# Hybrid decoder layer: part of the MLP's weight sums from transfers to VectorE, and an input loaded earlier and split later

## The chip, the cores and the metric

The kernel runs on one core of a Trainium2 chip. The metric is the device time of one execution in microseconds (us), as the median of several runs. The profile is one further execution, recorded by the hardware.

The engines are called as the profile calls them: PE is TensorE (matrix products; PEld is its loading of the stationary operand), DVE is VectorE, ACT is ScalarE, POOL is GpSimd, SP is the engine that issues most transfers. SBUF is the on-chip memory with 128 partitions, PSUM holds the products of TensorE in eight banks, DRAM is the large memory beside the core.

## The reference

One layer of a decoder for 512 tokens of 1024 numbers, all in fp32:

```python
proj = x @ w_in                                    # q, k, v of three mixers, and three gates
merged = (g[:, :, 0] * (o_da @ w_branch_da) + g[:, :, 1] * (o_sb @ w_branch_sb)
          + g[:, :, 2] * (o_dl @ w_branch_dil))    # g = sigmoid(gates)
x = layer_norm(DEEPNORM_ALPHA * x + merged @ w_out, ln1_g[i], ln1_b[i])
hid = jax.nn.relu(x @ w_up[i])                     # 1024 -> 4096
c = jnp.square(hid) @ w_down[i]                    # 4096 -> 1024
ple = jax.nn.sigmoid(x @ w_ple_gate[i]) * (p[i] @ w_ple[i])
x = layer_norm(DEEPNORM_ALPHA * x + c + ple, ln2_g[i], ln2_b[i])
```

`o_da`, `o_sb` and `o_dl` are a differential attention, a stick-breaking attention and a dilated sliding-window attention. For what follows the three products with large weights matter: the gates, the per-layer embedding (`ple`, with its input `p`) and the MLP (`w_up`, `w_down`).

## The kernel before

**Products in three parts.** Every fp32 operand of a large product is split into a high part (a cast to a shorter float, by ScalarE) and a low part (the remainder, by VectorE). The product is high times high, high times low and low times high, three matmuls that add up in a PSUM bank. For weights this is `split_next` (lines 239 to 262): ScalarE writes `wh` (line 255), VectorE writes `wl` (line 258). A weight block is 128 partitions x 1024 numbers, 512 KB.

**Buffers.** Raw blocks are loaded by SP into a ring of 5 (`RAW`, line 223), the split blocks lie in a ring of 7 (`RING`). `fill` issues the next load only when the block five loads earlier has no further use. `pump` splits ahead as far as `freed + RING` allows; `freed` grows by the blocks that an item lists as done.

**Items.** The work of TensorE is a list of items, each a group of matmuls with an eviction of its result. The loop at the end of `trunk` goes through them in order; at each item it evicts the result before, splits weights, calls hooks and may issue a transfer. The list has 59 items of projections, three gates of 14 items with the 8 items of branch 2 in front of the third gate, then the 8 items each of branch 0 and branch 1 (`first_branch` is the first of these), 8 of the output projection (`wout_at`), 22 of the embedding's gate and the embedding, and the MLP. The order of instructions within each engine's queue is set when the program is built; it follows the items by and large, with some instructions ahead of or behind their item.

**Seven products instead of eight.** The gates, the embedding's gate and the MLP multiply in blocks of two by two, with seven products (numbered 1 to 7) of sums of blocks instead of eight products of plain blocks. The four blocks of such a group are a quad here. Products 1, 2 and 3 use three raw blocks; products 4, 5, 6 and 7 use sums of blocks. The MLP has 15 quads: 8 of `w_up` and 7 of `w_down`; the last part of `w_down` is multiplied plainly.

**Where the sums are made.** `totals` (lines 149 to 174) puts them into two queues: `copies` (SP copies a raw block within DRAM, line 186) and `sums` (POOL starts a transfer that adds a block to the copy, line 190). A plain quad takes 4 copies and 4 sums and then loads 7 blocks: 3 raw ones and 4 sums. A mixed quad (`mixed=True`) takes 2 copies and 2 sums, for products 5 and 7; products 6 and 4 are then made by VectorE in place on the raw block of product 5: once it is split for product 5, another raw block is added to it (line 244). It loads 5 blocks. Gates 1 and 2 have mixed quads, gate 0, the embedding's gate and the whole MLP plain ones.

**When the sums are made.** The loop counts units of work (4 for a projection, 2 for a gate or a branch item) and calls `add` once per `rate` units. `add` takes a copy while fewer than 24 copies lead, else a sum. Until item 23 only copies are made. One sum waits for a cast three casts back, which spreads them.

**The MLP.** `mlp_items` takes `up` quad 0, then seven pairs of `up` quad b+1 and `down` quad b. `up_item` and `down` are its items, in the order of products 1, 2, 6, 5, 7, 3, 4 for `up`, and by the string `order` for `down`.

**The input p.** `load_pT` (lines 1250 to 1256) is called at item `first_branch + 6`. It loads the two halves of `pT` by SP, and at once casts each by ScalarE (line 1254) and subtracts by VectorE (line 1255). In the items around it `halves` (lines 571 to 575, hooked to `first_branch + 4` to `+ 7`) splits the four operands `oTh`, `oTl` of branch 1, by ScalarE and VectorE in turn for the cast (lines 93 and 95). The embedding's items (lines 784 to 806), which use the split `pT`, come after the output projection.

Of the kernel before, what the change touches and what calls it, by code (L numbers as in the profile page):

```python
# [52 lines left out]
def trunk(tc, a, out):  # L53
    nc = tc.nc
    es = ExitStack()
    with es:
# [92 lines left out]
        def totals(quads, mixed=False):  # L149

            def new():
                return dram.tile([P, 1024], F32, name=nm("total"), tag=nm("total"), bufs=1)

            if mixed:
                t = [(new(), new()) for _ in quads]
                for o in range(2):
                    for q, x in zip(quads, t):
                        copies.append((x[o], q[3 * o]))
                for o in range(2):
                    for q, x in zip(quads, t):  # L160
                        sums.append((x[o], q[1]))
                return [{1: q[0], 2: q[2], 3: q[3], 5: x[0], 7: x[1]} for q, x in zip(quads, t)]
            t = [[new() for _ in range(4)] for _ in quads]
            for o, i in ((0, 0), (2, 1), (1, 3), (3, 2)):
                for q, x in zip(quads, t):
                    copies.append((x[o], q[i]))
            for o, i in ((0, 1), (2, 3)):
                for q, x in zip(quads, t):
                    sums.append((x[o], q[i]))
            for o in (1, 3):  # L170
                for x in t:
                    sums.append((x[o], x[o // 2][:, :]))
            return [{1: q[0], 2: q[2], 3: q[3], 4: x[3], 5: x[0], 6: x[1], 7: x[2]} for q, x in zip(quads, t)]
# [658 lines left out]

        def mlp_items():
            nb = 7
            up_w, down_w = {}, {}

            def weights(b):
                q = [[a["wu"][b, i].rearrange("p j k m -> p (j k m)") for i in range(4)]]
                if b:
                    q.append([a["wd"][b - 1, i].rearrange("p k n -> p (k n)") for i in range(4)])  # L840
                w = totals(q)
                up_w[b] = w[0]
                if b:
                    down_w[b - 1] = w[1]
# [11 lines left out]
                nc.scalar.activation(t, src, AF.Relu)  # L856
                nc.scalar.activation(t, t, AF.Square)

            def up_item(b, p):
                c = chunk(up_w[b][p], 1024)  # L860

                def bank():
                    if p in (1, 2, 5):
                        held["A" if p == 1 else "B"] = mm_bank()
                    return held["B" if p in (2, 5, 3) else "A"]

                def mm(ps):
                    for j in range(2):
                        o = ps[:, 256 * j:256 * j + 256]
                        for k in range(4):  # L870
                            s = slice((4 * j + k) * P, (4 * j + k) * P + P)
                            h, lo = operand(x1_ops, p, k, slice(0, 256))
                            first = j == 0 and k == 0 and p in (1, 2, 5)
                            last = j == 1 and k == 3 and p in (2, 3, 4)
                            nc.tensor.matmul(o, c["h"][:, s], h, start=first, stop=False, skip_group_check=True)  # L875
                            nc.tensor.matmul(o, c["h"][:, s], lo, start=False, stop=False, skip_group_check=True)  # L876
                            nc.tensor.matmul(o, c["l"][:, s], h, start=False, stop=last, skip_group_check=True)  # L877

                def ev(ps):
                    if p in (1, 5, 6):  # L880
                        t = slot("cut")
                        nc.scalar.copy(t, ps)
                        cut[p] = t
                        return
                    if p == 2:
                        t = cut.pop(1)
                        nc.vector.tensor_add(t, t, ps)  # L887
                        squared(t, t)
                        n = 11
                    elif p == 7:  # L890
                        t = cut.pop(5)
                        nc.vector.tensor_sub(t, t, ps)
                        squared(t, t)
                        n = 22
                    elif p == 3:
                        t = cut.pop(6)
                        nc.vector.tensor_sub(t, ps, t)
                        squared(t, t)
                        n = 12
                    else:  # L900
                        t = slot("hid")
                        squared(t, ps)
                        n = 21
                    hid[b, n] = t
                    if n == 21:
                        jobs_of(b)
                item([c], mm, ev, need=[c], bank=bank, size=2)

            hid = {}

# [158 lines left out]
                    part(3, half, cc)  # L1069

            def ups(b):
                for p in (1, 2, 6, 5, 7, 3, 4):
                    up_item(b, p)
                    extra[len(items) - 1] = 2 if b == 1 else 1

            def downs(b):
                w = down_w[b]
                c = {}

                def go(p, r):  # L1080
                    if p not in c:
                        c[p] = chunk(w[p], 1024)
                    down(b, p, r, c[p], [c[p]] if r else [])

                order = "20 10 21 11 50 60 51 30 61 31 70 40 71 41" if b < nb - 1 else "10 11 50 60 51 61 70 71"
                for x in order.split():
                    go(int(x[0]), int(x[1]))
                if b == nb - 1:
                    for p in (2, 3, 4):
                        c[p] = chunk(w[p], 1024)  # L1090
                    return [c[p] for p in (2, 3, 4)]
# [157 lines left out]

        def load_pT():  # L1250
            for k in range(2):
                raw, h, lo = slot("pT"), slot("pTh", F32R), slot("pTl", F32R)
                nc.sync.dma_start(raw, a["pT"][:, k, :])
                nc.scalar.copy(h, raw)
                nc.vector.tensor_sub(lo, raw, h.bitcast(F32))
                pTs[k] = (h, lo)
# [336 lines left out]
        for n, it in enumerate(items):  # L1593
# [27 lines left out]
                turn_da()  # L1621
            if n >= 7 and not wout_at + 5 <= n < wout_at + 20 and not gates_at - 2 <= n < gates_at + 2:
                due[0] += it["size"]
                rate = 2.3 if n < gates_at else 5 if n < gates_at + 14 else 3 if n < first_branch else 2.2 if n < wout_at else 5.5
                while due[0] >= rate:
                    due[0] -= rate
                    add(n < 23)
            if n == first_branch + 6:
                load_pT()
            if n == wout_at - 6:  # L1630
                ln_consts("ln1_g", "ln1_b")
                for tt in range(4):
                    load_xn(tt)
# [110 lines left out]
```

## Time and profile before

| what | value |
|---|---|
| median of 3 runs | 1085.56 us (1085.28 to 1085.81) |
| the profiled execution's own time | 1085.31 us |
| its span in the profile | 1083.6 us |
| VectorE's casts and subtractions of weights, line 258 | 245, 296.5 us busy |
| copies within DRAM (SP) | 84 of 512 KB |
| adding transfers (POOL) | 84 of 512 KB |
| moved in all | 227.99 MB, 210 GB/s in the mean |

The span runs from the first to the last recorded instruction; the execution's own time is 1.7 us longer. Busy time is the time in which an engine executes; register, branch and transfer-issuing instructions are not counted in it. A row of waits reads: engine, instruction waiting, what ended the wait, then the total in us, how often, and the longest. A row of a timeline reads: start in us, duration, engine, line, operation, output and inputs, and in square brackets the idle time of the engine before it with what ended it. In the chain of waits each row is start, duration and what was running.

### The profile page before, as it was taken

How to read it: one execution, taken by the hardware profiler on the slowest of the kernel's cores; microseconds unless marked ns; L12 is line 12 of the kernel's file. 1: busy time of each engine (PE TensorE's matmuls, PEld its weight loads, DVE VectorE, ACT ScalarE, POOL GpSimd, SP SyncE). 2: the span in 40 equal slices, each digit the busy share in tenths (PEclk: the TensorE clock that was granted, in tenths of full speed). 3: DMA queues.
4: the chain of work that ended last, by engine and by line, in shares of the span. 5: the costliest groups of instructions: out<-in, count | busy, mean ns of one | idle time of the engine just before them, and what ended most of it. 6: DMA issues, size and time to landing. Idle time of an engine off the chain costs nothing.

```text
span 1083.6 us, 14812 instructions
## 1 busy us (share of the span) xinstructions
PE 1049.7 (97%) x5503; PEld 899.6 (83%) x5503; DVE 761.1 (70%) x1316; ACT 558.8 (52%) x908; POOL 98.1 (9%) x119
## 2 busy tenths in 40 slices
PE   9999999999999899999999969999999999999996
PEld 6877788999888688888887748877999889989985
DVE  6888566646354578887747745798786886787786
ACT  6566445333333446777536212275666566567551
POOL 0000101010211100111101100100001010110000
PEclk9999999999999899999999979999999999999999
DMA  7455564628979975475967984348779889898612
GB/s 272 155 214 184 206 251 91 144 97 214 271 205 310 272 224 175 116 214 160 321 176 248 289 301 136 109 140 260 252 237 285 250 243 280 233 273 237 224 68 78
DMA packets 69516, 227.99 MB, mean 210 GB/s; under 512 B 8077, under 2 KB 11037, under 8 KB 68100
## 3 DMA queue, kind: packets, MB, share of 16 engines
q1 hardware_dynamic: 45220, 179.97, 45.3%
q0 software_dynamic: 23648, 46.17, 24.3%
q8 instruction: 43, 0.70, 0.2%
q10 hardware_dynamic: 576, 0.92, 0.2%
q14 instruction: 29, 0.24, 0.1%
HBM read 224.90 MB, written 90.20 MB: 291 GB/s over the span
## 4 chain that ended last, share of the span: by engine, by line
PE 93%; DVE 3%; DMA 2%; ACT 1%; issue 1%; SPq 0%; POOL 0%; DVEq 0%; ACTq 0%
PE mm L84 6%; PE mm L85 6%; PE mm L86 6%; PE mm L875 5%; PE mm L876 5%; PE mm L877 5%; PE mm L363 3%; PE mm L365 3%; PE mm L364 3%; PE at L453 3%; PE at L454 3%; PE at L451 3%; PE mm L963 2%; PE mm L962 2%; PE mm L964 2%; PE mm L598 2%
## 5 line engine op out<-in xcount | busy, mean ns | idle before, releaser
L255 ACT CAST wh<-raw 128x1024 fp32r<-128x1024 f32 x245 | 255.4, 1050 | 242.4 <-PE mm L876 41.7
L258 DVE TENSOR_TENSOR wl<-raw,wh 128x1024 fp32r<-128x1024 f32 x245 | 296.5, 1222 | 117.4 <-ACT wh L255 114.1
L84 PE MATMUL mm<-xhT,wh 128*128 128x512 f32 x304 | 122.0, 401 | 1.3 <-DVE da_qb L105 1.1
L85 PE MATMUL mm<-xlT,wh 128*128 128x512 f32 x304 | 119.9, 394 | 0.0
L86 PE MATMUL mm<-xhT,wl 128*128 128x512 f32 x304 | 119.8, 394 | 0.0
L875 PE MATMUL mm<-XH,wh 128*128 128x256 f32 x256 | 72.6, 284 | 2.6 <-DVE cut L887 1.4
L876 PE MATMUL mm<-XL,wh 128*128 128x256 f32 x256 | 72.4, 283 | 0.0
L877 PE MATMUL mm<-XH,wl 128*128 128x256 f32 x256 | 72.4, 283 | 0.0
L84 PEld LDWEIGHTS mm<-xhT,wh 128*128 128x128 f32 x304 | 57.6, 190 | 15.3 <-issue 3.9
L86 PEld LDWEIGHTS mm<-xhT,wl 128*128 128x128 f32 x304 | 57.4, 189 | 12.2 <-DVE wl L258 0.3
L85 PEld LDWEIGHTS mm<-xlT,wh 128*128 128x128 f32 x304 | 57.7, 190 | 10.8
L363 PE MATMUL mm<-wh,xhT 128*128 128x512 f32 x160 | 64.2, 402 | 0.0
L190 POOL DMA_DIRECT2D total<-total x38 | 33.7, 894 | 328.2 <-ACT wh L255 286.1
L365 PE MATMUL mm<-wh,xlT 128*128 128x512 f32 x160 | 63.2, 395 | 0.0
L364 PE MATMUL mm<-wl,xhT 128*128 128x512 f32 x160 | 63.2, 395 | 0.0
L877 PE MATMUL mm<-xs,wl 128*128 128x256 f32 x192 | 54.3, 283 | 0.0
L875 PE MATMUL mm<-xs,wh 128*128 128x256 f32 x192 | 54.3, 283 | 0.0
L876 PE MATMUL mm<-xs,wh 128*128 128x256 f32 x192 | 54.3, 283 | 0.0
L875 PEld LDWEIGHTS mm<-XH,wh 128*128 128x128 f32 x256 | 49.1, 192 | 3.5 <-issue 1.6
L598 PE MATMUL mm<-wh,oTh 128*128 128x512 f32 x96 | 38.9, 405 | 12.9 <-DVE oTh L95 12.9
L876 PEld LDWEIGHTS mm<-XL,wh 128*128 128x128 f32 x256 | 49.1, 192 | 0.2
L877 PEld LDWEIGHTS mm<-XH,wl 128*128 128x128 f32 x256 | 49.1, 192 | 0.0
(421 smaller groups left out, 2550.2 us busy)
## 6 DMA issues: line engine op xcount, KB each, us to landing
raw<-total SPq DMA_DIRECT2D x84, 512.0 KB, 5.8
raw<-in_wt_dram SPq DMA_DIRECT2D x38, 512.0 KB, 7.4
total<-total POOLq DMA_DIRECT2D x38, 512.0 KB, 9.5
total<-in_wu_dram SPq DMA_DIRECT2D x32, 512.0 KB, 9.1
total<-in_wd_dram SPq DMA_DIRECT2D x28, 512.0 KB, 9.0
raw<-in_wd_dram SPq DMA_DIRECT2D x25, 512.0 KB, 5.3
raw<-in_wu_dram SPq DMA_DIRECT2D x24, 512.0 KB, 6.1
raw<-in_wv_dram SPq DMA_DIRECT2D x20, 512.0 KB, 4.0
```

The lines of the kernel that those rows point to most:

```text
L84: nc.tensor.matmul(ps, wh, xh, start=start, stop=False, skip_group_check=True)
L85: nc.tensor.matmul(ps, wh, xl, start=False, stop=False, skip_group_check=True)
L86: nc.tensor.matmul(ps, wl, xh, start=False, stop=stop, skip_group_check=True)
L255: i = nc.vector.tensor_copy(h, raw) if c.get("dve") else nc.scalar.copy(h, raw)
L258: i = nc.vector.tensor_sub(lo, raw, h.bitcast(F32))
L363: nc.tensor.matmul(ps, x1, c["h"][:, s], start=k == 0, stop=False)
L364: nc.tensor.matmul(ps, x1, c["l"][:, s], start=False, stop=False)
L365: nc.tensor.matmul(ps, x2, c["h"][:, s], start=False, stop=k == 7)
L598: nc.tensor.matmul(ps, h[:, q], c["h"][:, s], start=k == 0, stop=False)
L875: nc.tensor.matmul(o, c["h"][:, s], h, start=first, stop=False, skip_group_check=True)
L876: nc.tensor.matmul(o, c["h"][:, s], lo, start=False, stop=False, skip_group_check=True)
L877: nc.tensor.matmul(o, c["l"][:, s], h, start=False, stop=last, skip_group_check=True)
```

## The change

Quads of `up` 2, 4 and 6 and of `down` 1, 3 and 5 become mixed. `mixed_chunks` loads their five blocks (products 1 and 2, or 2 and 1, then 5, 3, 7) and splits in the order first two, 5, 6, 4, 3, 7, where 6 is block 5 with block 3 added and 4 is that with block 2 added. As this is not the order of the items, it also says which split blocks each item gives back: 5 and 6 after product 5 (in `down` after each), and 4, 3 and 7 after product 4. The rates of `add` change, and the input `pT` is loaded at `first_branch + 3` and split at `first_branch + 14`.

```diff
         def mlp_items():
             nb = 7
+            MIXED = (2, 4, 6)
             up_w, down_w = {}, {}
+
+            def mixed_chunks(w, first):
+                raw = {q: load(w[q], 1024) for q in (*first, 5, 3, 7)}
+                c = {p: chunk_of(raw[{6: 5, 4: 5}.get(p, p)], {6: raw[3], 4: raw[2]}.get(p))
+                     for p in (*first, 5, 6, 4, 3, 7)}
+                return c, {6: [], 5: [c[5], c[6]], 7: [], 3: [], 4: [c[4], c[3], c[7]]}
...
-                w = totals(q)
+                w = totals(q, b in MIXED)
...
-            def up_item(b, p):
-                c = chunk(up_w[b][p], 1024)
+            def up_item(b, p, c, free):
...
-                item([c], mm, ev, need=[c], bank=bank, size=2)
+                item(free, mm, ev, need=[c], bank=bank, size=2)
...
             def ups(b):
+                made, frees = mixed_chunks(up_w[b], (1, 2)) if b in MIXED else ({}, {})
                 for p in (1, 2, 6, 5, 7, 3, 4):
-                    up_item(b, p)
+                    c = made.get(p) or chunk(up_w[b][p], 1024)
+                    up_item(b, p, c, frees.get(p, [c]))
...
             def downs(b):
                 w = down_w[b]
-                c = {}
+                c, frees = mixed_chunks(w, (2, 1)) if b + 1 in MIXED else ({}, {})
+                if frees:
+                    frees[5], frees[6] = [c[5]], [c[6]]
...
-                    down(b, p, r, c[p], [c[p]] if r else [])
+                    down(b, p, r, c[p], frees.get(p, [c[p]]) if r else [])
...
         def load_pT():
             for k in range(2):
-                raw, h, lo = slot("pT"), slot("pTh", F32R), slot("pTl", F32R)
-                nc.sync.dma_start(raw, a["pT"][:, k, :])
+                pTs[k] = slot("pT")
+                nc.sync.dma_start(pTs[k], a["pT"][:, k, :])
+
+        def split_pT():
+            for k in range(2):
+                raw, h, lo = pTs[k], slot("pTh", F32R), slot("pTl", F32R)
                 nc.scalar.copy(h, raw)
                 nc.vector.tensor_sub(lo, raw, h.bitcast(F32))
                 pTs[k] = (h, lo)
...
-                rate = 2.3 if n < gates_at else 5 if n < gates_at + 14 else 3 if n < first_branch else 2.2 if n < wout_at else 5.5
+                rate = 2.4 if n < 23 else 3 if n < gates_at else 5 if n < gates_at + 14 else 3.5 if n < first_branch else 3 if n < wout_at else 5.5
...
-            if n == first_branch + 6:
+            if n == first_branch + 3:
                 load_pT()
+            if n == first_branch + 14:
+                split_pT()
```

## The prediction

> **What bounds the kernel now.** I read the page first (busy time, slices), then TensorE's waits, then the chain of waits around the longest of them, then single stretches by window.
>
> ```profile
> span 1083.6 us, 14812 instructions
> PE 1049.7 (97%) x5503; PEld 899.6 (83%) x5503; DVE 761.1 (70%) x1316; ACT 558.8 (52%) x908; POOL 98.1 (9%) x119
> PEclk9999999999999899999999979999999999999999
> ```
>
> TensorE is busy for 97% of the span and runs at full clock but for two slices. So work taken from another engine or from the transfers gives time only where TensorE waits. Its waits are few:
>
> ```profile
> PE mm L598 <- DVE oTh L95: 12.9, 1, 12.9
> PE at L1452 <- DVE dl_k L322: 2.8, 1, 2.8
> PE mm L875 <- DVE cut L887: 1.4, 1, 1.4
> PE at L453 <- DVE wl L258: 1.0, 1, 1.0
> ```
>
> One wait of 12.9 us stands out. The chain shows what it hangs on:
>
> ```profile
> 615.72 1.45 SPq L186
> 617.21 14.80 DMA pT<-in_pT_dram
> 632.09 0.63 ACT pTh L1254
> 632.74 0.69 DVE pTl L1255
> 633.43 0.35 DVE oTh L95
> 633.82 0.79 PE mm L598
> ```
>
> The second half of `pT` needs 14.80 us to land. ScalarE's cast of it (line 1254) stands at the head of its queue, VectorE's subtraction (1255) waits for the cast, and the last of branch 1's operands, `oTh` (line 95), is queued behind that subtraction. TensorE needs `oTh`; nobody needs `pT` until the per-layer embedding much later. It is pure queueing: early work behind a late transfer. TensorE then also pays in clock:
>
> ```profile
> 597.00:620.00 23.00, 23.00 (x102) 18.73 (x101) 18.51 (x26) 6.32 (x7) 4.41 (x5) 1.00 1.07 278
> 634.00:638.00 4.00, 4.00 (x10) 3.04 (x11) 2.92 (x5) 0.00 (x0) 0.00 (x0) 0.50 0.97 380
> 638.00:642.00 4.00, 4.00 (x22) 3.33 (x21) 1.67 (x4) 1.02 (x2) 0.00 (x0) 0.91 1.06 398
> ```
>
> The columns are the window, its length, busy time of PE, PEld, DVE, ACT, POOL, then granted clock, DMA share and GB/s. After the wait the clock is 0.50 for 4 us and 0.91 for 4 us: 4 x 0.50 + 4 x 0.09 = 2.4 us lost. The transfer was slow because the 16 DMA engines were full (share 1.07).
>
> **Part 1, pT loaded earlier and split later.** Removed: the wait of 12.9 us and the 2.4 us behind it, 15.3 us. Moved: two issues on SP's queue from item `first_branch + 6` to `+ 3`, and two casts and two subtractions to `+ 14`. I check each against its new neighbours.
>
> ```profile
> 594.60 0.39 PE L598 MATMUL mm<-wh,oTh 128*128 128x512 f32 x1
> ...
> 609.13 0.39 PE L598 MATMUL mm<-wh,oTh 128*128 128x512 f32 x1
> 611.85 0.39 PE L598 MATMUL mm<-wh,oTh 128*128 128x512 f32 x1
> ...
> 593.94 17.61 SPq L223 DMA_DIRECT2D raw<-in_wo_dram  x4
> 611.61 0.49 SPq L186 DMA_DIRECT2D total<-in_wd_dram  x1
> ...
> 615.17 0.50 SPq L1253 DMA_DIRECT2D pT<-in_pT_dram  x1
> ...
> 618.19 1.66 SPq L223 DMA_DIRECT2D raw<-in_wo_dram  x2
> ...
> 632.08 8.22 SPq L677 DMA_DIRECT2D xn<-in_xn_dram  x8
> ```
>
> An item of a branch is 12 matmuls; two matmuls twelve apart start 2.72 us apart. Item 0 of the branch begins at 594.6, so item 14 begins at 594.6 + 14 x 2.72 = 632.7 once the stall is gone. SP's queue is held by four weight loads (`raw<-in_wo`) until 611.6; the pT issues come behind them at 615.17 and 617.21 now. Three items earlier in the program they come ahead of the last two `wo` loads, so at the latest right after 611.6, the second 2.04 us later as now, and with the 14.80 us of the crowded engines they land by 611.6 + 2.0 + 14.8 = 628.4. ScalarE gets to the split at about 632.7: no wait. The four moved instructions are 2 x (0.63 + 0.69) = 2.6 us, half on each engine; ScalarE is busy for 6.32 of 23 us and VectorE for 18.51, so they fit. If that cover failed (an engine reaches the split 10 us early) ScalarE would idle some 6 us, and behind it would stand the weight casts of the output projection, which TensorE wants only from item 16. The two raw tiles stay in their slots for 11 items, but the four split tiles are taken eight items later, so fewer slots are held while branch 1's operands want theirs.
>
> What is late next? TensorE would come to the output projection 15.3 us sooner, with full DMA engines. The last of its weights are issued by 619.9, and they are for its second half. The residual `xn` is issued last, from 632.08 to 640.30:
>
> ```profile
> xn<-in_xn_dram SPq DMA_DIRECT2D x8, 256.0 KB, 5.3
> 663.25 0.69 DVE L700 SCALAR_TENSOR_TENSOR xn<-xn,mm 128x512 f32<-128x512 f32 x1 [1.32 <-PE mm L694]
> ```
>
> Its last tile lands at 640.3 + 5.3 = 645.6 even if SP gains nothing; the first use moves from 663.25 to 647.9. It holds with 2.3 us to spare, and only the first pair is wanted then. I take 15.3 us for this part, between 8.6 (15.3 less the 6.7 of rival 2) and 15.3.
>
> **Part 2, mixed quads in the MLP.** Six quads of seven weight blocks (`up` 2, 4, 6 and `down` 1, 3, 5) change. Removed for each: 2 copies on SP, 2 sums on POOL, and 2 of 7 block loads, so 12, 12 and 12 in all, each of 512 KB. Added: two VectorE additions each, 12. TensorE's matmuls stay. VectorE adds in place in the gates already:
>
> ```profile
> L244 DVE TENSOR_TENSOR raw<-raw,raw x8: 1216/1218/1226, 483.3 to 569.7; 128x1024 f32<-128x1024 f32 x8
> 572.10 1.23 DVE L258 TENSOR_TENSOR wl<-raw,wh 128x1024 fp32r<-128x1024 f32 x1 [1.17 <-ACT wh L255]
> 803.05:842.27 39.22, 39.22 (x253) 35.92 (x252) 30.27 (x37) 24.42 (x32) 3.53 (x4) 1.00 0.93 274
> L258 DVE TENSOR_TENSOR wl<-raw,wh 128x1024 fp32r<-128x1024 f32 x14 | 17.0, 1223 | 8.2 <-ACT wh L255 8.1
> ```
>
> One block pair (an `up` and a `down` quad) takes TensorE 39.22 us without a gap, and VectorE is busy for 30.27 of them. In the three changed pairs four additions bring 4 x 1.218 = 4.9 us: 35.1 of 39.22, so they lie beside TensorE, with 4.1 us left; 12 x 1.218 = 14.6 us in all cost nothing by throughput. But the sum is a chain: the addition waits for the block before it to be split, ScalarE's cast waits for the addition, and VectorE's own next subtraction waits for the cast (1.17 us idle in the row above). Evictions of PSUM banks are queued behind it on VectorE, and TensorE waits for those banks. The buffers also come back in groups (two after product 5, three after product 4), though each is free as soon as its readers are done. Seven ring buffers are about 7 x 2.8 = 19.6 us of TensorE's work ahead, against 4.9 us of additions per pair. In the gates eight such additions left one TensorE wait of 1.0 us (the row of L453 above). At that rate twelve cost 1.5 us. I take +1.5, between 0 and the saturated case (26 us, a rival below).
>
> A short wait may cost more than itself:
>
> ```profile
> 353.00:358.00 5.00, 2.23 (x11) 1.54 (x10) 1.99 (x5) 1.04 (x1) 0.88 (x1) 1.00 1.10 332
> 358.00:363.00 5.00, 5.00 (x21) 4.12 (x22) 3.44 (x27) 3.26 (x13) 0.00 (x0) 0.66 1.10 274
> 363.00:368.00 5.00, 4.04 (x20) 2.97 (x18) 2.69 (x15) 2.69 (x8) 0.00 (x0) 1.00 1.05 305
> 368.00:373.00 5.00, 3.92 (x18) 3.38 (x18) 4.62 (x10) 2.61 (x5) 2.73 (x3) 0.66 0.82 215
> ```
>
> The 2.8 us wait for `dl_k` falls in the first window, and in the next the clock is 0.66: 5 x 0.34 = 1.7 us on top. The Trainium skill (TensorE: Matmul & The Clock Gate, Part 1: The HAM clock gate) has the clock fall to half only after an idle window of about 3.4 us and come back after some 3.4 us of work. By that the 2.8 us wait would have had no price behind it, which this trace contradicts, and the big stall's would be an estimated 3.4 x 0.5 = 1.7 us instead of the 2.4 us seen, so the forecast 0.7 us higher.
>
> **Part 3, transfers.** Copies and sums fall from 84 + 84 to 72 + 72 and are issued more thinly from item 23 on (one per 3 units of work instead of 2.3, 3.5 instead of 3, 3 instead of 2.2). By counting the items, the sums issued when `up` 5 begins are 65 where 60 are needed (before: 76 where 68 were); that is the tightest place while sums are still being issued. A pair issues about five, so five are one pair ahead, 39 us.
>
> ```profile
> total<-total POOLq DMA_DIRECT2D x38, 512.0 KB, 9.5
> DMA to landing us min/median/max: 3.1/8.1/28.5
> ```
>
> The slowest transfer of a sum took 28.5 us, so no load will wait for one. The relief itself reaches TensorE only where a transfer ends a wait, and among the four waits above only the first does. The one at `dl_k` ends a chain of cast, subtraction and eviction:
>
> ```profile
> 354.93 1.04 ACT L255 CAST wh<-raw 128x1024 fp32r<-128x1024 f32 x1 [6.83 <-PE mm L85]
> 357.15 0.68 DVE L322 COPY dl_k<-mm 128x512 f32<-128x512 f32 x1
> ```
>
> The cast had waited 6.83 us for a buffer that TensorE held, not for a transfer. I take 0, between -8.2 (the whole disturbance of 353 to 373 goes when the engines' order there changes: 2.8 + 1.0 + 1.1 idle by the windows, 2 x 1.7 in clock) and +8.2 (another such arises).
>
> **Sum.** The profiled execution took 1085.31 us around its span of 1083.6; the median is 1085.56, 0.25 above. 1085.31 - 15.3 + 1.5 + 0 = 1071.5, and with the 0.25 about 1071.7.
>
> **Rivals.**
> 1. More goes than the stall: the thinner sums reshuffle the stretch at 353 and its 8.2 us vanish as well. For it: DMA share is above 1 there. Against: the chain there has no transfer. 1063.5.
> 2. Another wait takes the stall's place. With full DMA engines (share 1.07) and 15 us less time, `xn` or the output weights land about 5 us late, plus 1.7 us of clock, or a new disturbance like that at 353 appears elsewhere. Against: 2.3 us of slack and fewer transfers. 1071.7 + 6.7 = 1078.4.
> 3. Slower: VectorE becomes the bound in the changed pairs. If none of its 8.2 us of waits on ScalarE gives way to the additions, a pair needs 30.27 + 8.2 + 4.9 + 4 x 1.17 = 48.0 us instead of 39.22, three times 8.8 = 26.4 us: 1085.56 - 15.3 + 26.4 = 1096.7. It turns the result from 44.3 us of demand per pair on (15.3 / 3 = 5.1 above 39.22). For it: the in-order chain. Against: most of those waits are for buffers that TensorE frees one by one, and a queue that is behind no longer has them.
> 4. The change does not do what it says: the engines' order, fixed when the program is built, need not follow the items, and ScalarE still meets pT before it lands. The stall stays: 1085.56 + 1.5 = 1087.1.
>
> **How the numbers follow.** Forecast 0.70, rival 1 0.08, rival 2 0.10, rival 3 0.08, rival 4 0.04. The forecast's own range is 1068 to 1075 (no loss or twice 1.5 in the MLP, up to 2 us of lost slack at `xn`). The range 1063 to 1080 takes in rivals 1 and 2 and leaves out 3 and 4. A difference under 0.2% (2.2 us) is about what a measurement of this kernel cannot tell from none. Faster by more: 0.70 + 0.08 + 0.10 = 0.88; within: 0.04 (rival 4); slower: 0.08.
>
> **What would show it.** Part 1 is right if the wait of L598 for `oTh` is gone, no cast of pT waits for its transfer, and no slice near 620 to 640 shows a lower clock. Part 2 is right if VectorE is at about 35 of 39.2 us in three block pairs and TensorE still has no gap of over 1 to 2 us there; pairs longer than 39.2 us by several us mean rival 3. Part 3 is right if TensorE's gaps before the branches are about as they were. It is wrong if a new wait of several us stands ahead of the output projection, if line 1254's equivalent still waits for pT, or if new short waits with a clock of about 0.66 behind them are strewn over the span.

## The result, and the profile after

The changed kernel took 1075.8 us in the median of four runs (1074.75 to 1076.87), the kernel before 1085.59 us beside it (1085.28 to 1085.81). The ratio is 0.991 (95% interval 0.989 to 0.993): faster by 9.8 us. Forecast were 1071.7 us, a gain of 13.9 us, with a range of 1063 to 1080. The time is in the range, 4 us above the forecast, and just above the forecast's own range of 1068 to 1075.

The page of the changed kernel, busy time of each engine and TensorE's granted clock by slice:

```profile
span 1073.1 us, 14737 instructions
PE 1047.6 (98%) x5503; PEld 898.1 (84%) x5503; DVE 775.9 (72%) x1328; ACT 557.2 (52%) x908; POOL 87.2 (8%) x107
PEclk9999999999999999999999999999999999999999
```

VectorE has 12 instructions and 14.8 us more (12 x 1.22 us), POOL 12 instructions less. The slices of 8 and 7 are gone from the clock. TensorE's waits in the changed kernel (line numbers from the MLP on are some 6 to 14 higher than before):

```profile
PE at L1466 <- DVE dl_k L322: 2.8, 1, 2.8
PE mm L881 <- DVE xn L975: 2.5, 3, 0.8
PE mm L598 <- ACT oTh L93: 1.7, 1, 1.7
PE mm L600 <- DVE oTl L574: 1.6, 1, 1.6
```

The wait of 12.9 us is gone and `dl_k` is as it was. Three rows are new: two at the branches, for `oTh` and `oTl`, and one in the MLP, three times 0.8 us for `xn`. The row of L453 is gone.

To see where the time went, the span is cut at the first matmul of each stage. These rows of the changed kernel give the cuts (the first of the two times is the start of the first instruction, the second that of the last):

```profile
L84 PE MATMUL mm<-xhT,wh x304: 387/389/774, 17.5 to 440.8; 128*128 128x512 f32 x152
...
L451 PE MATMUL at<-wh,xhT x48: 389/389/475, 442.2 to 585.2; 128*128 128x512 f32 x48
L451 PE MATMUL mm<-wh,xhT x48: 387/389/477, 448.9 to 590.6; 128*128 128x512 f32 x48
...
L692 PE MATMUL mm<-wh,XH x64: 389/389/482, 643.0 to 688.6; 128*128 128x512 f32 x64
...
L1011 PE MATMUL mm<-wh,hh x10: 389/389/390, 1034.4 to 1052.6; 128*128 128x512 f32 x10
```

So the projections go from 17.5 to 442.2, the gates to 590.6 (the last such matmul of the third gate), the two branches to 643.0, output projection, embedding and MLP to 1034.4, and the plain last part to the end. The lengths in us, with the same cuts in the kernel before:

| stage | before | after | difference |
|---|---|---|---|
| until the first projection | 17.9 | 17.5 | -0.4 |
| projections, attentions | 425.8 | 424.7 | -1.1 |
| gates | 150.2 | 148.4 | -1.8 |
| branches 0 and 1 | 62.8 | 52.4 | -10.4 |
| output projection to MLP | 388.3 | 391.4 | +3.1 |
| plain part | 38.6 | 38.7 | +0.1 |
| span | 1083.6 | 1073.1 | -10.5 |

**The branches.** The stall that was forecast away is away: pT's two transfers are issued at 600.5 and 601.2 instead of 615.2 and 617.2, and nothing waits for them. The transfers and the casts in the changed kernel:

```profile
L1263 SPq DMA_DIRECT2D pT<-in_pT_dram x2: 377/474/572, 600.5 to 601.2; - x2
L1268 ACT CAST pTh<-pT x2: 621/622/624, 649.6 to 650.1; 128x512 fp32r<-128x512 f32 x2
```

But the stage is 10.4 us shorter, not 15.3. The operands of branch 1 are late by themselves now. The chain of waits of the changed kernel at the start of branch 1 (start, duration, what ran):

```profile
611.94 1.06 ACT wh L255
...
613.03 0.31 DVE wl L258
...
614.17 0.68 DVE gt L604
614.85 1.14 DVE wl L258
615.99 0.60 DVE gt L608
616.59 0.61 DVE oTl L574
...
617.25 0.80 PE mm L600
618.04 0.43 PE mm L598
```

TensorE waits for `oTl` behind two weight subtractions and two evictions on VectorE. Behind the wait its matmuls are 0.43 us apart instead of 0.23; the granted clock from 617 to 621 us is 0.57. When the operands are made stands in the timelines. First ScalarE in the kernel before, then ScalarE and VectorE in the changed one:

```profile
595.11 0.62 ACT L93 CAST oTh<-oT 128x512 fp32r<-128x512 f32 x1
...
597.95 0.60 ACT L93 CAST oTh<-oT 128x512 fp32r<-128x512 f32 x1
```

```profile
611.94 1.05 ACT L255 CAST wh<-raw 128x1024 fp32r<-128x1024 f32 x1 [8.46 <-PE mm L600]
...
614.29 1.14 ACT L93 CAST oTh<-oT 128x512 fp32r<-128x512 f32 x2
```

```profile
616.51 0.69 DVE L574 TENSOR_TENSOR oTl<-oT,oTh 128x512 fp32r<-128x512 f32 x1
...
617.56 1.29 DVE L574 TENSOR_TENSOR oTl<-oT,oTh 128x512 fp32r<-128x512 f32 x2
...
619.23 0.69 DVE L574 TENSOR_TENSOR oTl<-oT,oTh 128x512 fp32r<-128x512 f32 x1
```

Before, ScalarE's two of the four casts ran at 595 and 598, some 20 us ahead of use (branch 1 begins at 616.6), and only the last operand hung on pT. Now all four pairs are made from 614 to 620, just when TensorE wants them. Nothing makes these casts wait at that moment: ahead of them in ScalarE's queue stands a weight cast that waits for TensorE, with 8.46 us of idle time until 611.94. So they are late by their place in the queue, which is set when the program is built.

**The MLP.** Three block pairs in the changed kernel, of which the second is a changed one (`up` 2 and `down` 1); the ends 807.99 and 887.48 are the ends of two of the three waits for `xn` (columns as in the prediction's windows):

```profile
768.77:807.99 39.22, 38.39 (x247) 34.92 (x245) 35.13 (x43) 25.09 (x35) 3.52 (x4) 1.00 0.72 213
807.99:847.74 39.75, 39.75 (x256) 36.45 (x257) 32.54 (x38) 23.56 (x33) 4.40 (x5) 1.00 0.84 229
847.74:887.48 39.74, 38.91 (x250) 35.45 (x249) 32.55 (x38) 24.68 (x33) 4.43 (x5) 1.00 0.82 223
```

VectorE is never the bound: it is busy for 32.54 of 39.75 us in the changed pair and for at most 35.13 of 39.22. That 35.13 is the figure of the forecast is chance: the forecast counted four additions in a changed pair, but VectorE makes those of an `up` quad ahead, in the pair before, so each of these windows holds two (2.4 us), and the first has more of the other work. From one wait's end to the next two pairs take 39.75 + 39.74 = 79.49 us instead of 2 x 39.22 = 78.44, so some 1.05 more, three times. At the head of each mixed `up` quad TensorE waits 0.8 us; the remaining 0.2 us per quad is not explained. What stands before it on VectorE, and on ScalarE:

```profile
801.35 1.23 DVE L244 TENSOR_TENSOR raw<-raw,raw 128x1024 f32<-128x1024 f32 x1
...
803.75 3.50 DVE L258 TENSOR_TENSOR wl<-raw,wh 128x1024 fp32r<-128x1024 f32 x3 [0.58 <-ACT wh L255]
807.16 0.68 DVE L975 TENSOR_TENSOR xn<-xn,mm 128x512 f32<-128x512 f32 x1
```

```profile
802.66 2.95 ACT L255 CAST wh<-raw 128x1024 fp32r<-128x1024 f32 x3 [2.66 <-DVE raw L244]
```

The second addition of the mixed `up` quad that is about to begin (801.35; in m2_up below, which has no mixed `down` quad, it stands in the same place) holds up ScalarE's casts; three of them come at once, and their three subtractions (3.50 us) are queued ahead of the eviction of the last product of the `down` quad before (line 975, 807.16). TensorE's next `up` product needs that bank, and starts at 807.99.

### The profile page after: what moved, and what is told of

Its sections match the earlier page's. It is cut to its first block, busy times and chain, and to the rows that moved or that the text cites. A ratio compares the mean times of both kernels' runs of the same rounds, so it can differ in the third digit from the quotient of the medians.

```text
span 1073.1 us, 14737 instructions
## 1 busy us (share of the span) xinstructions
PE 1047.6 (98%) x5503; PEld 898.1 (84%) x5503; DVE 775.9 (72%) x1328; ACT 557.2 (52%) x908; POOL 87.2 (8%) x107
## 4 chain that ended last, share of the span: by engine, by line
PE 95%; DVE 3%; ACT 1%; issue 1%; DMA 0%; POOL 0%; DVEq 0%; SPq 0%; ACTq 0%
PE mm L84 6%; PE mm L85 6%; PE mm L86 6%; PE mm L881 5%; PE mm L882 5%; PE mm L883 5%; PE mm L363 3%; PE mm L365 3%; PE mm L364 3%; PE at L451 3%; PE at L453 3%; PE at L454 3%; PE mm L968 2%; PE mm L969 2%; PE mm L970 2%; PE mm L600 2%
## 5 line engine op out<-in xcount | busy, mean ns | idle before, releaser
L190 POOL DMA_DIRECT2D total<-total x26 | 23.9, 936 | 279.9 <-ACT wh L255 264.5
L365 PEld LDWEIGHTS mm<-wh,xlT 128*128 128x128 f32 x160 | 38.0, 238 | 3.8
```

Source lines behind the costliest of these rows:

```text
L365: nc.tensor.matmul(ps, x2, c["h"][:, s], start=False, stop=k == 7)
```

## The experiments

The main theory: what is missing of the 15.3 us is a new wait at branch 1, made by where pT's tiles are asked for in the program; the MLP costs what stands at the head of the mixed `up` quads; the thinner rates shorten the gates. The rivals: the additions as such cost the time, or the transfers' rates. Ten kernels were run, each beside the kernel before on the same chip (medians of before 1085.7 to 1086.9):

| kernel | pT loaded at first_branch + | mixed quads | rates | median us | ratio (95%) | projections | gates | branches | to MLP's end |
|---|---|---|---|---|---|---|---|---|---|
| before | 6 | none | old | 1085.6 | 1 | 425.8 | 150.2 | 62.8 | 388.3 |
| after | 3 | 3 up, 3 down | thin | 1075.8 | 0.991 (0.989 to 0.993) | 424.7 | 148.4 | 52.4 | 391.4 |
| e1_pt_only | 3 | none | old | 1075.2 | 0.990 (0.988 to 0.991) | 426.1 | 150.2 | 53.0 | 388.0 |
| e2_load8 | 8 | 3 up, 3 down | thin | 1071.1 | 0.986 (0.984 to 0.988) | 424.8 | 148.4 | 47.0 | 391.4 |
| s3_load5 | 5 | 3 up, 3 down | thin | 1071.7 | 0.987 (0.985 to 0.989) | 424.6 | 148.5 | 48.4 | 391.5 |
| f1_pt8_only | 8 | none | old | 1072.3 | 0.986 (0.985 to 0.988) | 426.0 | 150.2 | 47.2 | 389.7 |
| e4_mixed_only | 6 | 3 up, 3 down | old | 1096.9 | 1.010 (1.008 to 1.011) | 427.1 | 150.2 | 69.7 | 391.6 |
| e5_old_rates | 3 | 3 up, 3 down | old | 1080.5 | 0.995 (0.993 to 0.996) | 427.1 | 150.2 | 53.7 | 391.5 |
| m1_down | 3 | 6 down | thin | 1074.7 | 0.989 (0.987 to 0.990) | 424.7 | 148.4 | 53.6 | 388.4 |
| m2_up | 3 | 6 up | thin | 1078.2 | 0.992 (0.990 to 0.994) | 424.8 | 148.4 | 52.3 | 393.6 |
| m3_down_load8 | 8 | 6 down | thin | 1069.4 | 0.984 (0.982 to 0.986) | 427.1 | 148.4 | 47.1 | 388.3 |
| r1_plain_thin | 8 | none | thin | 1104.7 | 1.017 (1.015 to 1.020) | 427.0 | 148.4 | 46.9 | 423.4 |

The last four columns are the lengths of the stages in each kernel's profile, cut as above. All kernels but before and e4_mixed_only split pT at `first_branch + 14`.

### pT alone

The kernel before, with pT's load and split as in the changed kernel and nothing else:

```diff
-                raw, h, lo = slot("pT"), slot("pTh", F32R), slot("pTl", F32R)
-                nc.sync.dma_start(raw, a["pT"][:, k, :])
+                pTs[k] = slot("pT")
+                nc.sync.dma_start(pTs[k], a["pT"][:, k, :])
+        def split_pT():
...
-            if n == first_branch + 6:
+            if n == first_branch + 3:
                 load_pT()
+            if n == first_branch + 14:
+                split_pT()
```

> Only the load and the split of pT are moved as in the change; quads and rates are those of before. Theory: the early raw tiles of pT take the first two free slots, so the operands of branch 1 (oTh, oTl) are made some 17 us later than before and TensorE waits for them at the start of branch 1: the 12.9 us wait goes, 3.3 us of waits and 1.6 us of lower clock take its place, a gain of 10.4 and about 1075.2 us. Rival: the late operands come from the thinner sums or the mixed quads (another order of the engines), not from pT: then no such wait here, a gain of 15.3 and about 1070.3 us.

It took 1075.2 us, as much as the whole change, and its branches 53.0 us. The two new waits are there, to the tenth:

```profile
PE mm L598 <- ACT oTh L93: 1.7, 1, 1.7
...
PE mm L600 <- DVE oTl L574: 1.6, 1, 1.6
```

With plain quads and old rates they come all the same: they belong to pT's move, not to the transfers or the MLP.

### pT loaded later

The changed kernel with the load at `+ 8`, behind the last of the hooks that split branch 1's operands (`+ 4` to `+ 7`), and then with the load at `+ 5`, between them:

```diff
-            if n == first_branch + 3:
+            if n == first_branch + 8:
                 load_pT()
```

> The changed kernel with pT loaded at first_branch + 8, behind the operands of branch 1 in the program, instead of + 3; split at + 14 as before. Theory (the slots): the operands are made early again, the two waits of 1.7 and 1.6 us at the start of branch 1 and the lower clock behind them go, 4.9 us less, about 1070.9 us. Rival (another cause of the order): the waits stay, 1075.8 us. If pT then lands after ScalarE reaches its cast, a wait for its transfer shows again, a few us.

> The changed kernel with pT loaded at first_branch + 5 instead of + 3 (split still at + 14). Theory: tiles are asked for in program order, and pT's two raw tiles hold up every later request until they get their slots, the four pairs of branch operands of branch 1 among them. Two items later in the program, the requests of operands 0 and 1 stand ahead of pT's and those of 2 and 3 behind: so two of the four subtractions for oTl run early (595 to 602 us on the changed kernel's clock) and two late (614 to 620), TensorE's waits at lines 598 and 600 (1.7 and 1.6 us in the changed kernel) become one shorter wait of 0 to 2 us, one or two matmuls of the order later, and the branch stage is between 47.0 (load at + 8) and 52.4 us (load at + 3): 48 to 51, time 1071.5 to 1074.5. Rival A, it is the number of slots held or the time at which pT's transfer runs, not the order of requests: all four operands stay late and both waits stay, 1075 to 1077. Rival B, any later load is enough: no wait, branch stage 47.0, 1070 to 1072.

With `+ 8` the branches take 47.0 us, 5.4 less than with `+ 3`, and both waits are gone: that is the price of the new wait, 3.3 us of waiting and most of the rest behind it at lower clock. Over all kernels the stage takes 52.3 to 53.7 us with `+ 3` and 46.9 to 47.2 with `+ 8`. With `+ 5` they take 48.4 us, and the waits are small:

```profile
PE mm L598 <- ACT oTh L93: 0.4, 1, 0.4
...
PE mm L600 <- DVE oTl L574: 0.2, 1, 0.2
```

In s3_load5 two of the four subtractions for `oTl` run early and two late, where the changed kernel had all four late. VectorE in s3_load5:

```profile
591.74 0.68 DVE L574 TENSOR_TENSOR oTl<-oT,oTh 128x512 fp32r<-128x512 f32 x1
...
594.53 0.69 DVE L574 TENSOR_TENSOR oTl<-oT,oTh 128x512 fp32r<-128x512 f32 x1
```

```profile
617.24 0.69 DVE L574 TENSOR_TENSOR oTl<-oT,oTh 128x512 fp32r<-128x512 f32 x1
...
618.29 0.69 DVE L574 TENSOR_TENSOR oTl<-oT,oTh 128x512 fp32r<-128x512 f32 x1
```

So the number of early operands follows the place of the load among the hooks: none at `+ 3`, two at `+ 5`, three at `+ 6` (the kernel before), four at `+ 8`. (The time of s3_load5 alone, 1071.7 us, would fit its rival B too; the two late operands and the two small waits do not.) The reading that fits all four places: pT's tiles and the operands are of one kind of buffer (`slot`, 46 of them), these are handed out in program order while the program is built, and a request that must wait for a buffer holds up every later request, whoever makes it. If only the count of buffers mattered, pT's two raw tiles could have displaced two tiles, one operand; they displaced eight. What is shown is the effect of the place. That it works through the buffers is an inference: no run changed their number, and why pT's own request waited that long is open. The pT tiles are the cheapest to be late (their split comes at `+ 14`), and `+ 3` put them ahead of the most urgent ones.

### The mixed quads alone

The kernel before, with the changed quads, but with pT and rates as before:

```diff
+            MIXED = (2, 4, 6)
...
-                w = totals(q)
+                w = totals(q, b in MIXED)
```

> Only the six mixed quads; pT and the rates are those of before, so the wait of 12.9 us stays. Theory: at the head of each mixed up quad three subtractions of weights stand in VectorE's queue ahead of the eviction of the last down item, and TensorE waits 0.8 us and loses 1.05 us, three times: about 3.2 us slower than before, 1088.8 us. Rival: the small waits in the MLP come from the later sums (the rates): then 1085.6 us.

It took 1096.9 us, 1% more than before, where a loss of a few us was expected. The MLP is as expected (391.6 us, 3.3 more than before). The rest is the old stall, which grew from 12.9 to 19.7 us: TensorE's wait, the chain and a window of e4_mixed_only.

```profile
PE mm L598 <- DVE oTh L95: 19.7, 1, 19.7
```

```profile
621.64 18.79 DMA pT<-in_pT_dram
```

```profile
624.00:645.00 21.00, 2.75 (x7) 2.10 (x8) 3.44 (x6) 1.24 (x2) 1.78 (x2) 0.58 1.08 284
```

pT's second half needs 18.79 us here, with the DMA engines full (1.08), instead of 14.80. Fewer transfers in all made more adding ones at this place: SP issues the last of its 72 copies at 616.19, just ahead of pT, where the kernel before has copies until 811.5. So at the old rates the copies are used up by this place in the program, and `add`, which takes a copy or else a sum, has only sums left. POOL starts nine adding transfers between 602.4 and 612.8; in the kernel before it started two from 602 to 613. That these adding transfers are what slowed pT is not shown, and one run speaks against it: e5_old_rates (below) starts nine as well, from 602.8 to 613.3, and its halves of pT landed in 11.5 and 13.0 us. What is shown is that the mixed quads without the other two parts lose 10.4 us (1096.9 against 1086.5 of before beside it).

### The rates

The changed kernel with the rates of before:

```diff
-                rate = 2.4 if n < 23 else 3 if n < gates_at else 5 if n < gates_at + 14 else 3.5 if n < first_branch else 3 if n < wout_at else 5.5
+                rate = 2.3 if n < gates_at else 5 if n < gates_at + 14 else 3 if n < first_branch else 2.2 if n < wout_at else 5.5
```

> The changed kernel with the rates of before. In the two profiles the changed kernel is 3.3 us ahead when the first branch begins (1.5 before the gates, 1.8 in the gates). Theory: the thinner sums give these 3.3 us: about 1079.1 us here, with TensorE's wait of 1 us in the last gate back. Rival: they come from the reshuffled order alone and the rates do nothing: 1075.8 us.

1080.5 us. The gates take 150.2 us again. All five kernels with the old rates have 150.2 in the table, the seven with the thin ones 148.4 or 148.5, with pT at 3, 5 or 8 and quads of every kind. So the thin rates are worth 1.8 us in the gates. 1.0 of it is the wait at line 453, which stands ahead of the branches in the traces of all five kernels with the old rates and in none of the seven with the thin ones; the way from the rate to that wait stays open. Another 1.3 us against the changed kernel are in the branches (53.7; m1_down has 53.6 with the thin rates, so this is not theirs), and 3.7 us lie ahead of the gates, of which 2.8 us can come without any edit, as two runs of one program show (below).

The reverse: do the thin rates need the mixed quads? The kernel before with pT at `+ 8` and the thin rates, all quads plain:

```diff
-                rate = 2.3 if n < gates_at else 5 if n < gates_at + 14 else 3 if n < first_branch else 2.2 if n < wout_at else 5.5
+                rate = 2.4 if n < 23 else 3 if n < gates_at else 5 if n < gates_at + 14 else 3.5 if n < first_branch else 3 if n < wout_at else 5.5
...
-            if n == first_branch + 6:
+            if n == first_branch + 8:
```

> The kernel before with pT loaded at + 8 and split at + 14, and with the changed kernel's thinner rates of copies and sums, but all fifteen quads summed by transfers (no additions in the MLP). Theory: the thin rates are what shortens the gate stage from 150.2 to 148.4 us, and the mixed quads are what makes them possible: without them 168 instead of 144 copies and sums have to go out, so at the thin rates they fall behind the loads, which then force sums out late and wait for them; TensorE gets waits for block loads in the output projection or the first MLP blocks, 3 us or more in all, and the time is 1072 to 1080. Rival: the quads' due times leave enough room, the gate stage is 148.4 and nothing waits in the MLP, whose stretch is that of plain quads (about 388.4 by the same anchor): 1069 to 1071.5, as good as the best so far, and the VectorE additions were of no use.

They do, and more than expected: 1104.7 us, 19 us above the kernel before beside it and 32 above f1_pt8_only, from which it differs by the rates alone. Gates and branches are short (148.4 and 46.9), but the MLP loses 35.1 us against the kernel before. The engines now wait for the sums. ScalarE's wait for loads of sums, TensorE's largest wait, and a stretch of the chain of r1_plain_thin:

```profile
ACT wh L255 <- DMA raw<-total: 29.1, 8, 9.5
```

```profile
PE mm L875 <- DVE cut L887: 7.5, 2, 6.0
```

```profile
920.97 13.23 DMA total<-total
...
934.67 9.94 DMA total<-total
...
946.19 10.80 DMA raw<-in_wd_dram
```

ScalarE waits for loads of sums 8 times; in the kernel before and the changed one no such wait stands among ScalarE's. Two adding transfers, one after the other, and a load behind them hold the chain for 34 us. TensorE's waits after the branches add up to 25.6 us (2.7 before); the rest of the increase goes with the clock, which was 0.87 to 0.96 in windows of 40 us from 860 to 1020. That is the use of VectorE's additions: with them 144 copies and sums have to be made instead of 168, and the thin rates are enough.

### Where the mixed quads lie

The changed kernel with six mixed quads again, but all of `down` (0 to 5), and all of `up` (1 to 6):

```diff
-            MIXED = (2, 4, 6)
+            UP, DOWN = (), (0, 1, 2, 3, 4, 5)
...
-                made, frees = mixed_chunks(up_w[b], (1, 2)) if b in MIXED else ({}, {})
+                made, frees = mixed_chunks(up_w[b], (1, 2)) if b in UP else ({}, {})
...
-                c, frees = mixed_chunks(w, (2, 1)) if b + 1 in MIXED else ({}, {})
+                c, frees = mixed_chunks(w, (2, 1)) if b in DOWN else ({}, {})
```

> The changed kernel with the six mixed quads all among the down quads (0 to 5), none among the up quads; as many additions, copies and sums as in the changed kernel. Theory (the head of a mixed up quad): the three waits of 0.8 us for the eviction of the last down item vanish, the stretch from the output projection to the plain part is 389.6 us as before the change instead of 392.8, 3.2 us less in all, about 1072.6 us. Rival (the price lies in VectorE's additions themselves): twelve additions as before, the stretch stays at about 392.8 and the time at 1075.8 us.

> The changed kernel with the six mixed quads all among the up quads (1 to 6), none among the down quads. Theory (the head of a mixed up quad): six such waits instead of three, the stretch is 389.6 + 6 x 1.05 = 395.9 us, about 1079 us in all. Rival (the additions themselves): 392.8 and 1075.8 us.

The number of additions is the same in all three kernels. With `down` alone the MLP takes 388.4 us, as with no mixed quads at all (388.3), and no wait at the eviction is left. With `up` alone it takes 393.6, and the wait stands five times instead of three:

```profile
PE mm L880 <- DVE xn L974: 4.1, 5, 0.8
```

So the additions cost nothing; the eviction queued behind them at the head of a mixed `up` quad does, about 1 us each time (3.1 / 3 in the changed kernel, 5.3 / 5 in m2_up). The sixth quad of m2_up, `up` 1, follows `up` 0 and not a `down` quad, so no such eviction stands ahead of it. The time of m1_down is 1074.7 us, 2.1 above what was expected, although its MLP is 3.0 us shorter than the changed kernel's as expected: in its profile the gates begin 2.2 us later (444.4 instead of 442.2) and the branches are 1.2 us longer.

### Both repairs, and pT alone at + 8

The changed kernel with six mixed `down` quads and pT loaded at `+ 8`, and the kernel before with nothing but pT loaded at `+ 8` and split at `+ 14`:

> Both repairs together: pT loaded at first_branch + 8 and the six mixed quads among the down quads. By the stages of the profiles: 4.9 to 5.4 us less for the operands of branch 1 and 3.2 us less in the MLP than the changed kernel, about 1067.5 us. If the price of the additions does not depend on the place: 1070.5 us.

> The kernel of before with pT alone moved (load at first_branch + 8, split at + 14): plain quads, the rates of before. Theory: the whole of the stall goes, 15.3 us, and nothing else, about 1070.2 us; so mixed quads and rates together would be worth nothing beside it. Rival (the transfers are too crowded for this without the fewer sums): another wait of several us between the first branch and the output projection, 1074 to 1080 us.

m3_down_load8 is the fastest kernel at 1069.4 us, 1.6% under before and 1.9 us above what was expected; its branches (47.1), gates (148.4) and MLP (388.3) are each within 0.3 us of the shortest. f1_pt8_only has 1072.3: without any of the mixed quads or rates, 14.6 of m3_down_load8's 17.5 us are there (both against the 1086.9 of before beside them). Its MLP is 1.4 us longer than before; a wait of 0.7 us at line 453 after the branches stands in its trace, and the rest stays open. The intervals of the two overlap a little (0.982 to 0.986, 0.985 to 0.988), and the spans of the two profiles are 1069.6 and 1069.0 us, so that m3_down_load8 is the faster of them is likely, not certain.

## Why the prediction was right or wrong

**The main stall: right, and its size too.** 15.3 us were to go. With pT out of the way altogether (load at `+ 8`) the branches are 62.8 - 47.2 = 15.6 us shorter in f1_pt8_only and 62.8 - 47.0 = 15.8 in e2_load8. The wait, the 2.4 us of clock behind it and the forecast that nothing else is late at the output projection hold: neither `xn` nor an output weight is among TensorE's waits there. Two steps on the way came out otherwise without effect: pT was issued some 11 us earlier than its latest time in the prediction (600.5 instead of 611.6), and ScalarE came to the split at 649.6 instead of about 632.7. And the reason given for the slow transfer, full DMA engines at a share of 1.07, is not enough by itself: in r1_plain_thin the halves of pT landed in 8.3 us in the median at a share of 1.11.

**Where it failed.** "The two raw tiles stay in their slots for 11 items, but the four split tiles are taken eight items later, so fewer slots are held while branch 1's operands want theirs." This counted slots, where the order of the requests decides. Moving pT's load from `+ 6` to `+ 3` moved its two requests past all the operands' hooks that had stood ahead of it, and the operands, early until then, were held up behind them. The prediction checked SP's queue, ScalarE's and VectorE's time, and not the order in which buffers are asked for. By its own sign part 1 is right only in part: TensorE still waits for `oTh` at line 598, for 1.7 us instead of 12.9. In the sum the term is the 15.3, which measured 10.4 in the changed kernel: 15.8 for the stall less 5.4 for the new wait.

**Rival 2 by half.** It said that another wait would take the stall's place, for 6.7 us. One did, 5.4 us, but not from `xn` or the weights of the output projection, which it named; only its last words, a new disturbance elsewhere, cover it, without a cause. It had a chance of 0.10 and priced the right thing with the wrong cause.

**The MLP.** The throughput was right: VectorE does not bound a pair, and twelve additions of 1.22 us cost nothing (m1_down). The figure of 35.1 us for a changed pair was not: it is 32.54, as half of its additions are made in the pair before. The mechanism was named, evictions queued behind the additions, but sized from the gates' single wait of 1.0 us for eight additions, so 1.5 us. Measured were 3.1. The price is by mixed `up` quads behind a `down` quad (about 1 us each), not by additions. Rival 3, VectorE as the bound, did not occur.

**The transfers.** 0 was forecast; 1.8 us came from the thin rates in the gates. The prediction had the row for 1.0 of it, L453's wait, but took it as the price of additions in place, while the rates decide whether it comes. The larger point was not in the forecast at all: the three parts are not independent. Mixed quads at the old rates, with the old pT, are 10.4 us slower than before (e4_mixed_only); the thin rates without mixed quads cost 32 us (r1_plain_thin against f1_pt8_only). That no load waits for a sum held for the changed kernel.

**The clock behind a short wait.** The 2.8 us wait for `dl_k` stayed, and in the window behind it the changed kernel again has less than full clock:

```profile
357.00:362.00 5.00, 4.60 (x18) 4.03 (x19) 3.96 (x28) 2.75 (x11) 0.00 (x0) 0.66 1.09 272
...
367.00:372.00 5.00, 3.83 (x22) 2.83 (x22) 4.89 (x12) 3.13 (x5) 1.87 (x2) 1.00 0.46 79
```

But the second fall, ten us later, is missing (1.00 where before had 0.66), and the projections are 1.1 us shorter. That it is an effect of the change is not shown. m1_down and m3_down_load8 are one program up to the branches: in the traces all engines run the same instructions in the same order, and the transfers are issued in the same order. Their windows behind the same wait, first m1_down, then m3_down_load8:

```profile
359.20:364.20 5.00, 4.60 (x19) 4.18 (x20) 3.96 (x28) 2.71 (x11) 0.00 (x0) 0.66 1.14 287
364.20:369.20 5.00, 4.04 (x20) 3.00 (x18) 2.40 (x14) 2.92 (x10) 0.00 (x0) 1.00 0.36 133
```

```profile
359.60:364.60 5.00, 4.61 (x15) 4.03 (x16) 3.96 (x28) 2.71 (x11) 0.00 (x0) 0.50 1.09 272
364.60:369.60 5.00, 5.00 (x22) 4.10 (x21) 1.17 (x7) 1.49 (x8) 0.00 (x0) 0.85 0.41 147
```

The clock of the one is back at 1.00 after 5 us, that of the other stays at 0.82 to 0.85 for 15 us more, and the projections take 424.7 and 427.1 us. So the same program pays different prices for the same wait, and what sets them stays open. The Trainium skill's rule (TensorE: Matmul & The Clock Gate, Part 1: The HAM clock gate), a fall only after some 3.4 us of idle time, is contradicted here as it was in the kernel before, by the 0.66 behind an idle time of 2.8 us.

**The sum.** -10.4 + 3.1 - 1.8 - 1.5 = -10.6 us against 10.5 measured in the spans. The last term is the start and the projections. No work of the engines is changed there, only the pace and the order of copies and sums, and two runs of one program differ there by more. So the forecast is as near as it is in part by luck: 4.9 us less from the branches and 1.6 us more in the MLP than forecast are offset by 1.8 us from the gates and these 1.5 us, which the forecast put at nothing.

## What to carry to other kernels

When a step is moved in the program, ask which queues it is moved past, and check the order of requests for buffers among them: here a tile with time to spare was best asked for behind the urgent ones. Before an engine takes over work from transfers, look at what is queued behind the new work at each place (here an eviction at the head of one kind of quad); the place decides, not the amount. Work that is taken from a pool which a pacing rule draws on changes what that rule does next, so try such parts together and apart.

## What the runs showed of the hardware

The start differs between runs by more than some of the effects studied: the first projection matmul began at 17.5 us in the changed kernel and at 20.2 in e2_load8, which is the same program up to the branches; over all kernels it began at 17.3 to 20.2. To the start of the gates the two need 442.2 and 445.0 us, and m1_down and m3_down_load8, also one program up to there, 444.4 and 447.2. The later stages repeat much better: the gates took 148.4 us in six traces with the thin rates. So effects of one or two microseconds are read from the stages here, where the medians blur them.

An adding transfer of 512 KB (`total<-total` on POOL's queue) took 9.3 us in the changed kernel's median and 10.2 in r1_plain_thin's, but 13.23 us once in r1_plain_thin's chain, and a half of pT with 256 KB took 14.80 us in the kernel before and 18.79 us in e4_mixed_only, where the DMA share was 1.08 from 624 to 645. A full share alone does not set this time: the median of pT's two halves was 8.3 us in r1_plain_thin with a share of 1.11 from 619.6 to 628.
